# DeltaNet's element-wise work off GpSimd, and its projections summed in one set of PSUM columns

## The chip, the cores and the metric

The kernel runs on one core of a Trainium2 chip. The metric is the device time of one execution in microseconds (us); the time before is the median of three runs. TensorE (PE) multiplies, VectorE (DVE) and ScalarE (ACT) do element-wise work from SBUF and PSUM, GpSimd (POOL) does element-wise work in SBUF and issues its own DMAs, and SyncE (SP) issues the loads of the weights.

## What is computed

One decoder block on 256 tokens of width 2048: an input norm, two mixers side by side (sparse attention, NSA, and a gated DeltaNet), gates that merge them, an output projection with a residual, a SwiGLU feed-forward and a last norm. The change touches DeltaNet alone, whose reference, cut to what matters, is this:

```python
def gated_deltanet(qkv, z, a, beta_logit, conv_w, a_log, dt_bias, norm_w):
    qkv = silu(causal_depthwise_conv(qkv, conv_w))          # 4 taps
    q, k, v = split into 8 heads of 128
    q = l2norm(q) * dk ** -0.5
    k = l2norm(k)
    gc = jnp.cumsum(chunks(gdec), axis=-1)
    decay = jnp.exp(jnp.where(lower_incl, gc[..., :, None] - gc[..., None, :], -jnp.inf))
    lmat = jnp.where(strict, jnp.einsum('bhnid,bhnjd->bhnij', kb, k) * decay, 0.0)
    tinv = lax.linalg.triangular_solve(eye + lmat, eye, left_side=True, lower=True)
    ...
    o = rms_norm(o, norm_w) * jax.nn.silu(z)
```

## The kernel before

**The weight stream.** Nearly all the time goes into products of 256 tokens with some 270 MB of weights. The weights come in chunks of 1 MB (`load`, L122, three buffers `raw`). Each half of a chunk is split by `split` (L133) in two parts for the reduced-precision matmul: ScalarE copies `hi` (L141), VectorE subtracts to get `lo` (L142), with three buffers of each. The activations are kept as `hi` and `lo` parts too. A product is the sum of hi·hi, hi·lo and lo·hi. `group_t` (L180) makes 256 output columns, transposed, out of two chunks: for each piece of 128 rows and each of two feature tiles, one matmul of 512 columns multiplies the weights' `hi` with both parts of the activations (L196), and one of 256 columns the weights' `lo` with the activations' `hi` (L197). A half-chunk has eight such pairs. The two sums stand in different PSUM columns, so ScalarE copies the one to SBUF (L200, `ev`) and VectorE adds the other to it (L202).

**The lanes.** The mixers are written as generators. After every half-chunk, `pump` takes one more piece from each of three lanes, so that the mixers' work stands between the weights' products. `split` is issued at a raised priority, so that `hi` and `lo` stand ahead of the mixers' work on ScalarE and VectorE where they can; `pin` keeps an instruction no earlier on its engine than where it is written. Each engine works through its own list in order: a waiting instruction holds up all behind it.

**DeltaNet.** Six groups of 512 features (k, k, v, v, q, q; L1054 and after), each two calls of `group_t`, are scaled by the input norm's factor into `pre` (`conv_in`, L344). `conv_taps` (L347) takes the first of four taps as a product (L353) and adds three (L355), all on VectorE, then ScalarE applies silu. `dn_small` makes the decay factors `E` on GpSimd (subtraction, mask before the exponential and mask after it, L326, L327, L335); `prep_k` multiplies them by 1/|k| (L390) and with the keys' products into `MT` (L402). `solve` inverts 64 diagonal blocks of 32 x 32: the blocks go through DRAM (`scrM`) into `Lb` with a block on each partition; GpSimd masks the rest of `MT` (L430), scales `Lb` (L435), takes 31 steps of a product (L441) and a difference (L443), and copies the transpose (L446); the inverses go back through DRAM (`scrT`, `scrTT`) into `D` and `DT`. `dn_main` waits for all of it, multiplies the gate `zs` by the output norm's weight on GpSimd (L510), and makes the products `P`, `U` and the state's. `dn_norm` scales the output and multiplies it by the gate on GpSimd (L636), and `dn_out` transposes it into `odn`.

**After it.** NSA's keys and queries go through `rope` (L655) on GpSimd. Later stages (merge gates, output projection, feed-forward) use the same `group_t` and `group` and aren't changed.

Of the kernel before, what the change touches and what calls it, by code (L numbers as in the profile page):

```python
# [14 lines left out]
P = 128  # L15
# [78 lines left out]
class Kern:  # L94
# [50 lines left out]
    def group(self, srcs, acts, w=512, first=None, t_outer=False):  # L145
        """one group of w output columns, tokens on partitions: out[tok, w] in ps[t][:, :w]

        t_outer: the last three half-chunks serve the first 128 tokens before the others."""
# [31 lines left out]
    def group_t(self, srcs, acts, out=None):  # L180
        """one group of 256 output columns, transposed: out[f*128.., tok] is the sum of
        ps[:, f, 0, :] (both products with the hi parts of the activations) and ps[:, f, 1, :]"""
# [21 lines left out]

    def hilo(self, out, v):
        """out[:, 0] + out[:, 1] = v, in two parts for the products"""
        self.hilo2(out[:, 0], out[:, 1], v)
# [19 lines left out]
    def rsqrt(self, v, shape, tag):  # L227
        """1/sqrt(v) in float32: a first guess from the bits and Newton steps."""
# [10 lines left out]
    def pin(self, ins):  # L239
        """no earlier on its engine than where it is written"""  # L240
        return self.tc.keep_in_program_order(ins)
# [8 lines left out]
    def bc(self, col, n):  # L250
        """[P, a] -> [P, a, n]"""
        a = col.shape[1]
        return col.unsqueeze(2).to_broadcast([P, a, n])

    # ================= DeltaNet =================
    def dn_small(self, ab):
# [47 lines left out]
        # decay factors, transposed: E[j, i] = exp(gc_i - gc_j) for i >= j, else 0  # L304
        up = self.cs["utri"][:, None, :].to_broadcast([P, 4, 128])
# [13 lines left out]
        for i in range(len(order) + 3):  # L319
            if i < len(order):  # L320
# [3 lines left out]
                if t == 0:  # L324
                    self.pin(nc.gpsimd.tensor_tensor(self.kd[:, hs], E[:, :, 127], self.gc[:, 0, hs], op=OP.subtract))
                self.pin(nc.gpsimd.tensor_tensor(E.ap, E.ap, self.bc(self.gc[:, t, hs], 128), op=OP.subtract))  # L326
                self.pin(nc.gpsimd.tensor_tensor(E.ap, E.ap, up, op=OP.mult))  # L327
            if i >= 3:
                t, hg = order[i - 3]
# [5 lines left out]
                self.pin(nc.gpsimd.tensor_tensor(E.ap, E.ap, up, op=OP.mult))  # L335
            yield

    def conv_in(self, e, half, pre):
        """rows of a group, scaled, where the causal conv reads them: [128 ch, 4, 3 + 256 tok]"""
# [7 lines left out]
    def conv_taps(self, pre, cT, feat0):  # L347
        """causal conv over 4 feature tiles, then silu"""
        nc, V = self.nc, self.nc.vector
        cw = self.sm["cw"]  # L350
        for f in range(4):
            o = (feat0 + f) * 4
            V.tensor_scalar(cT[:, f, :], pre[:, f, 0:256], cw[:, o:o + 1], None, op0=OP.mult)  # L353
# [9 lines left out]
    def prep_k(self, pre, cT, hg):  # L363
# [14 lines left out]
        # 1/|k| goes into the decay factors, the row scales and the keys for the state  # L378
# [9 lines left out]
        for t in range(2):  # L388
            E = self.E[t, hg]
            nc.gpsimd.tensor_tensor(E.ap, E.ap, self.bc(rk[:, t, :], 128), op=OP.mult)  # L390
# [14 lines left out]
    def solve(self):  # L405
        """inverses of the 32x32 diagonal blocks of I + L, blocks on partitions"""
# [22 lines left out]
        # off-diagonal blocks only, for the products  # L429
        nc.gpsimd.tensor_tensor(self.MT.ap, self.MT.ap, self.cs["offmask"][:, None, :].to_broadcast([P, 16, 128]), op=OP.mult)  # L430
# [4 lines left out]
        nc.gpsimd.tensor_tensor(Lb[:64], Lb[:64], bb[:64, None, :].to_broadcast([64, 32, 32]), op=OP.mult)  # L435
        yield
        prf = pr[:64].rearrange("p a b -> p (a b)")
        for j in range(31):
            n, m = 31 - j, j + 1
            pv = prf[:, :n * m].rearrange("p (a b) -> p a b", b=m)  # L440
            nc.gpsimd.tensor_tensor(pv, Lb[:64, j, j + 1:32].unsqueeze(2).to_broadcast([64, n, m]),  # L441
                            Tb[:64, j, 0:m].unsqueeze(1).to_broadcast([64, n, m]), op=OP.mult)
# [876 lines left out]
```

## Time and profile before

| what | value |
|---|---|
| median of 3 runs | 1530.34 us (1530.16 to 1530.35) |
| span of the profiled execution, first to last instruction | 1526.5 us |
| TensorE matmul, busy | 1491.8 us (98%) |
| VectorE, busy | 989.9 us (65%) |
| ScalarE, busy | 713.1 us (47%) |
| GpSimd, busy | 248.8 us (16%) |

How to read the rows below. A row of waits has the engine and tile that waited, then the one waited for, and the time in all, the number of times and the longest, in us. A row of windows has the window (us from the span's start), its length, then the busy time (and number of instructions) of TensorE's matmuls, its weight loads, VectorE, ScalarE and GpSimd, the granted TensorE clock as a share of the full one, the DMA share and GB/s. A row of a timeline has the start, the duration, engine, line, operation, output and inputs, the shape and the number; in brackets the idle time before it and what ended it. A row of groups has line, engine, operation, output and inputs, shapes and number, then the busy time in us and the mean of one in ns, then the idle time before them. A matmul's end is modelled, so starts tell more than durations.

### The profile page before, as it was taken

How to read it: one execution, taken by the hardware profiler on the slowest of the kernel's cores; microseconds unless marked ns; L12 is line 12 of the kernel's file. 1: busy time of each engine (PE TensorE's matmuls, PEld its weight loads, DVE VectorE, ACT ScalarE, POOL GpSimd, SP SyncE). 2: the span in 40 equal slices, each digit the busy share in tenths (PEclk: the TensorE clock that was granted, in tenths of full speed). 3: DMA queues.
4: the chain of work that ended last, by engine and by line, in shares of the span. 5: the costliest groups of instructions: out<-in, count | busy, mean ns of one | idle time of the engine just before them, and what ended most of it. 6: DMA issues, size and time to landing. Idle time of an engine off the chain costs nothing.

```text
span 1526.5 us, 20516 instructions
## 1 busy us (share of the span) xinstructions
PE 1491.8 (98%) x8199; PEld 1290.8 (85%) x8199; DVE 989.9 (65%) x1321; ACT 713.1 (47%) x910; POOL 248.8 (16%) x197
## 2 busy tenths in 40 slices
PE   6999999999999999999999999999999999999997
PEld 6988778988888888888888888888888888888886
DVE  7688998578877865676666555555565555455444
ACT  4654433344455545554454444444444444344343
POOL 5140695233500000030000000000000000000000
PEclk8999999999999999999999999999999999999999
DMA  6645446335654455555545555555555555555553
GB/s 230 220 170 184 145 146 190 114 138 184 231 182 152 155 187 181 183 181 189 185 174 193 192 180 183 190 193 180 182 190 193 180 183 217 193 193 194 193 193 110
DMA packets 40943, 276.74 MB, mean 181 GB/s; under 512 B 4992, under 2 KB 5008, under 8 KB 9232
## 3 DMA queue, kind: packets, MB, share of 16 engines
q1 hardware_dynamic: 38592, 268.34, 50.5%
q10 hardware_dynamic: 1152, 4.46, 0.8%
q0 software_dynamic: 1104, 2.64, 0.7%
q8 instruction: 64, 1.05, 0.3%
q14 instruction: 31, 0.25, 0.0%
HBM read 272.52 MB, written 2.89 MB: 180 GB/s over the span
## 4 chain that ended last, share of the span: by engine, by line
PE 90%; DVE 6%; POOL 1%; issue 1%; ACT 1%; DMA 0%; SPq 0%; DVEq 0%; ACTq 0%; POOLq 0%
PE mm L196 40%; PE mm L197 20%; PE mm L218 8%; PE mm L219 8%; PE mm L217 8%; DVE lo L142 3%; DVE main L355 1%; PE U L534 1%; PE oacc L862 1%; ACT hi L141 0%; POOL main L662 0%; DMA xs<-in_xT 0%; PE pt L848 0%; POOL ys L664 0%; DVE zsg L344 0%
## 5 line engine op out<-in xcount | busy, mean ns | idle before, releaser
L142 DVE TENSOR_TENSOR lo<-raw,hi 128x1024 fp32r<-128x1024 f32 (+2 forms) x512 | 649.4, 1271 | 468.6 <-ACT hi L141 464.1
L141 ACT ACTIVATE hi<-raw 128x1024 fp32r<-128x1024 f32 (+2 forms) x512 | 535.5, 1047 | 735.6 <-PE mm L196 430.1
L196 PE MATMUL mm<-h,hi 128*128 128x512 f32 x1408 | 497.7, 397 | 0.0
L196 PE MATMUL mm<-hh,hi 128*128 128x512 f32 x1152 | 415.1, 402 | 0.0
L197 PE MATMUL mm<-h,lo 128*128 128x256 f32 x1408 | 395.8, 281 | 0.0
L197 PE MATMUL mm<-hh,lo 128*128 128x256 f32 x1152 | 326.0, 283 | 11.1 <-DVE lo L142 11.0
L196 PEld LDWEIGHTS mm<-h,hi 128*128 128x128 f32 x1408 | 264.7, 188 | 65.2
L197 PEld LDWEIGHTS mm<-h,lo 128*128 128x128 f32 x1408 | 264.3, 188 | 0.0
L196 PEld LDWEIGHTS mm<-hh,hi 128*128 128x128 f32 x1152 | 217.9, 189 | 50.5 <-issue 0.2
L197 PEld LDWEIGHTS mm<-hh,lo 128*128 128x128 f32 x1152 | 217.7, 189 | 14.2 <-DVE lo L142 14.0
L1167 POOL TENSOR_TENSOR sgt<-sgt,R 128x512 f32<-128x512 f32 x22 | 39.5, 1798 | 544.4 <-ACT sgt L1166 544.4
L219 PE MATMUL mm<-hi,fxy 128*128 128x512 f32 x192 | 75.6, 394 | 0.0
L218 PE MATMUL mm<-lo,fxy 128*128 128x512 f32 x192 | 75.3, 392 | 0.0
L217 PE MATMUL mm<-hi,fxy 128*128 128x512 f32 x192 | 74.5, 388 | 0.0
L219 PE MATMUL mm<-hi,fa 128*128 128x512 f32 x160 | 63.0, 394 | 0.0
L218 PE MATMUL mm<-lo,fa 128*128 128x512 f32 x160 | 62.7, 392 | 0.0
L217 PE MATMUL mm<-hi,fa 128*128 128x512 f32 x160 | 62.1, 388 | 0.0
L202 DVE TENSOR_TENSOR ev<-mm,ev 128x512 f32<-128x512 f32 x88 | 60.1, 683 | 0.0
L1106 POOL TENSOR_TENSOR main<-main 128x512 f32<-128x512 f32 x7 | 14.1, 2015 | 267.3 <-DVE main L1105 267.3
L200 ACT ACTIVATE ev<-mm 128x512 f32<-128x512 f32 x96 | 55.9, 582 | 0.0
L217 PE MATMUL mm<-hi,hh 128*128 128x354 f32 (+2 forms) x128 | 46.8, 366 | 5.8 <-ACT hh L972 5.8
L218 PE MATMUL mm<-lo,hh 128*128 128x354 f32 (+2 forms) x128 | 46.4, 362 | 6.0 <-DVE lo L142 6.0
(345 smaller groups left out, 1698.7 us busy)
## 6 DMA issues: line engine op xcount, KB each, us to landing
raw<-in_wfg SPq DMA_DIRECT2D x88, 1024.0 KB, 4.8
raw<-in_wd SPq DMA_DIRECT2D x44, 1024.0 KB, 4.8
raw<-in_wmg SPq DMA_DIRECT2D x32, 1024.0 KB, 4.9
raw<-in_wdn SPq DMA_DIRECT2D x24, 1024.0 KB, 4.9
raw<-in_nsa SPq DMA_DIRECT2D x16, 1024.0 KB, 4.9
raw<-in_wo SPq DMA_DIRECT2D x16, 1024.0 KB, 4.8
raw<-in_wud SPq DMA_DIRECT2D x8, 1024.0 KB, 4.8
raw<-in_wun SPq DMA_DIRECT2D x8, 1024.0 KB, 4.9
```

The costliest lines, as they stand in the source:

```text
L141: nc.scalar.activation(hv, rv[:, m * h:m * h + m, :], AF.Copy)
L142: nc.vector.tensor_tensor(lv, rv[:, m * h:m * h + m, :], hv.bitcast(F32), op=OP.subtract)
L196: nc.tensor.matmul(ps[:, f], hv[:, k, fs], a, start=begin, stop=False, skip_group_check=True)
L197: nc.tensor.matmul(ps[:, f, 0, :], lv[:, k, fs], a[:, 0, :], start=False, stop=last, skip_group_check=True)
L200: nc.scalar.activation(e[:], ps[:, :, 1, :], AF.Copy)
L202: nc.vector.tensor_tensor(out, ps[:, :, 0, :], e[:], op=OP.add)
L217: nc.tensor.matmul(o, a[:, 0, sl], hv[:, k, :], start=begin, stop=False)
L218: nc.tensor.matmul(o, a[:, 0, sl], lv[:, k, :], start=False, stop=False)
L219: nc.tensor.matmul(o, a[:, 1, sl], hv[:, k, :], start=False, stop=last)
L355: V.scalar_tensor_tensor(cT[:, f, :], pre[:, f, j:j + 256], cw[:, o + j:o + j + 1], cT[:, f, :], op0=OP.mult, op1=OP.add)
L534: nc.tensor.matmul(bv[:, j, :], Pm[t, hg][:, j, :], U[t, hg][:, j, :], start=True, stop=True)
L1167: nc.gpsimd.tensor_tensor(sgt[:], sgt[:], self.R2b, op=OP.mult)
```

## The change

- The decay factors are made on VectorE, one head at a time: a subtraction and a minimum with zero in one instruction, then the exponential on ScalarE. The masks go; the mask is applied once, in the product with 1/|k|.
- In the solve, the mask of `MT` (in four pieces, one per half-chunk), the scaling of `Lb` and the 62 steps move to VectorE, with more yields between the steps, and the transposed copy moves to ScalarE.
- The gate's product with the norm's weight goes; the weight is brought onto the partitions as `dnwc` and applied where `dn_out` evacuates the transposed output. In `dn_norm`, scale and gate are one VectorE instruction per head.
- DeltaNet's projections use `group_s`: three products of 256 columns into the same PSUM columns, with no addition after them; `conv_in` reads PSUM.
- The first tap of the convolution is an activation on ScalarE.
- `rope` may take its buffer from another free region.

```diff
+    def group_s(self, srcs, acts):
+        ps = self.pmain.tile([P, 2, 256], F32, tag="mm", name=self.nm("mm"))
...
+                    for f in range(2):
+                        fs = slice(f * P, f * P + P)
+                        nc.tensor.matmul(ps[:, f], hv[:, k, fs], a[:, 0, :], start=begin and f == 0, stop=False, skip_group_check=True)
+                        nc.tensor.matmul(ps[:, f], hv[:, k, fs], a[:, 1, :], start=False, stop=False, skip_group_check=True)
+                        nc.tensor.matmul(ps[:, f], lv[:, k, fs], a[:, 0, :], start=False, stop=last, skip_group_check=True)
+                self.pump()
+        return ps[:]
...
-        for i in range(len(order) + 3):
+        for i in range(len(order) + 1):
...
-                self.pin(nc.gpsimd.tensor_tensor(E.ap, E.ap, self.bc(self.gc[:, t, hs], 128), op=OP.subtract))
-                self.pin(nc.gpsimd.tensor_tensor(E.ap, E.ap, up, op=OP.mult))
+                for j in range(4):
+                    h = hg * 4 + j
+                    self.pin(V.tensor_scalar(E[:, j, :], E[:, j, :], self.gc[:, t, h:h + 1], 0.0, op0=OP.subtract, op1=OP.min))
...
                 self.pin(nc.scalar.activation(E.ap, E.ap, AF.Exp))
-                self.pin(nc.gpsimd.tensor_tensor(E.ap, E.ap, up, op=OP.mult))
...
-            V.tensor_scalar(cT[:, f, :], pre[:, f, 0:256], cw[:, o:o + 1], None, op0=OP.mult)
+            self.pin(nc.scalar.activation(cT[:, f, :], pre[:, f, 0:256], AF.Copy, scale=cw[:, o:o + 1]))
...
-            nc.gpsimd.tensor_tensor(E.ap, E.ap, self.bc(rk[:, t, :], 128), op=OP.mult)
+            for j in range(4):
+                V.scalar_tensor_tensor(E[:, j, :], E[:, j, :], rk[:, t, j:j + 1], self.cs["utri"], op0=OP.mult, op1=OP.mult)
...
-        nc.gpsimd.tensor_tensor(self.MT.ap, self.MT.ap, self.cs["offmask"][:, None, :].to_broadcast([P, 16, 128]), op=OP.mult)
...
-        nc.gpsimd.tensor_tensor(Lb[:64], Lb[:64], bb[:64, None, :].to_broadcast([64, 32, 32]), op=OP.mult)
+        for q in range(4):
+            self.pin(V.tensor_tensor(self.MT[:, 4 * q:4 * q + 4, :], self.MT[:, 4 * q:4 * q + 4, :],
+                                     self.cs["offmask"][:, None, :].to_broadcast([P, 4, 128]), op=OP.mult))
+            yield
+        self.pin(V.tensor_tensor(Lb[:64], Lb[:64], bb[:64, None, :].to_broadcast([64, 32, 32]), op=OP.mult))
...
-            nc.gpsimd.tensor_tensor(pv, Lb[:64, j, j + 1:32].unsqueeze(2).to_broadcast([64, n, m]),
-                            Tb[:64, j, 0:m].unsqueeze(1).to_broadcast([64, n, m]), op=OP.mult)
-            nc.gpsimd.tensor_tensor(Tb[:64, j + 1:32, 0:m], Tb[:64, j + 1:32, 0:m], pv, op=OP.subtract)
-            if j % 2 == 2 - 1:
+            self.pin(V.tensor_tensor(pv, Lb[:64, j, j + 1:32].unsqueeze(2).to_broadcast([64, n, m]),
+                                     Tb[:64, j, 0:m].unsqueeze(1).to_broadcast([64, n, m]), op=OP.mult))
+            self.pin(V.tensor_tensor(Tb[:64, j + 1:32, 0:m], Tb[:64, j + 1:32, 0:m], pv, op=OP.subtract))
+            if j % 2 or 7 < j < 23:
                 yield
-        nc.gpsimd.tensor_copy(pr[:64], Tb[:64].rearrange("p a b -> p b a"))
+        self.pin(nc.scalar.activation(pr[:64], Tb[:64].rearrange("p a b -> p b a"), AF.Copy))
...
-        zv = self.zs.ap.rearrange("p t (h d) -> p (t h) d", d=128)
-        self.pin(nc.gpsimd.tensor_tensor(zv, zv, self.sm["dnw"][:, None, :].to_broadcast([P, 16, 128]), op=OP.mult))
+        V.tensor_tensor(dg.ap, self.sm["dnw"], self.cs["ident"], op=OP.mult)
+        V.tensor_reduce(self.dnwc[:], dg.ap, axis=AX.X, op=OP.add)
...
-        V.tensor_tensor(o.ap, o.ap, self.bc(r[:], 128), op=OP.mult)
-        nc.gpsimd.tensor_tensor(o.ap, o.ap, self.zs[:, t, hg * 512:hg * 512 + 512].rearrange("p (a b) -> p a b", b=128), op=OP.mult)
+        for j in range(4):
+            V.scalar_tensor_tensor(o[:, j, :], o[:, j, :], r[:, j:j + 1], self.zs[:, t, hg * 512 + j * P:hg * 512 + (j + 1) * P], op0=OP.mult, op1=OP.mult)
...
-        nc.scalar.activation(oh, bv, AF.Copy)
-        V.tensor_tensor(ol, bv, oh.bitcast(F32), op=OP.subtract)
+        nc.scalar.activation(oh, bv, AF.Copy, scale=self.dnwc[:])
+        V.scalar_tensor_tensor(ol, bv, self.dnwc[:], oh.bitcast(F32), op0=OP.mult, op1=OP.subtract)
...
-        t = self.ar.alloc([2, 256])
+        t = self.ar.alloc([2, 256], "my")
...
-                e = self.group_t([t["wdn"][(g * 2 + half) * 2 + c] for c in range(2)], hact)
+                e = self.group_s([t["wdn"][(g * 2 + half) * 2 + c] for c in range(2)], hact)
```

**Where instructions move.** VectorE in the middle of the solve, before: the first taps (L353), the additions of the evacuation (L202), and no solve.

```order
L142 TENSOR_TENSOR lo_1851<-raw_1816,hi_1850 128x1024
L142 TENSOR_TENSOR lo_1885<-raw_1882,hi_1884 128x1024
L202 TENSOR_TENSOR ev_1811<-mm_1698,ev_1811 128x512
L344 TENSOR_TENSOR zsg<-ev_1811,R_427 128x2x256
L353 TENSOR_SCALAR main<-zsg,smalls 128x256
L142 TENSOR_TENSOR lo_1910<-raw_1882,hi_1909 128x1024
```

The same stretch of VectorE now (L365 is `conv_in`, L466 and L468 are a step's product and difference, L376 the later taps):

```order
L142 TENSOR_TENSOR lo_2315<-raw_2253,hi_2314 128x1024
L376 SCALAR_TENSOR_TENSOR main<-zsg,smalls,main 128x256
L466 TENSOR_TENSOR xs<-xs 64x256
L364 MEMSET zsg 128x4x3
L365 TENSOR_TENSOR zsg<-mm_2108,R_427 128x2x256
L142 TENSOR_TENSOR lo_2347<-raw_2344,hi_2346 128x1024
L468 TENSOR_TENSOR xs<-xs 64x16x16
L466 TENSOR_TENSOR xs<-xs 64x255
L468 TENSOR_TENSOR xs<-xs 64x15x17
L466 TENSOR_TENSOR xs<-xs 64x252
L468 TENSOR_TENSOR xs<-xs 64x14x18
L142 TENSOR_TENSOR lo_2377<-raw_2344,hi_2376 128x1024
```

Up to five steps of the solve now stand between two `lo`, and `conv_in` takes its operand from the PSUM tile `mm`. Earlier on VectorE, where the blocks have just been sent to DRAM, now (L457 is a piece of the mask of `MT`, L460 the scaling of `Lb`; the pieces of the mask wait for the DMAs that read `MT`, and L460 for those that fill `Lb` and `bb`):

```order
L457 TENSOR_TENSOR main<-main,consts 128x512
L142 TENSOR_TENSOR lo_1862<-raw_1819,hi_1861 128x1024
L457 TENSOR_TENSOR main<-main,consts 128x512 x3
L142 TENSOR_TENSOR lo_1904<-raw_1901,hi_1903 128x1024
L460 TENSOR_TENSOR xs<-xs,bb_1664 64x1024
L365 TENSOR_TENSOR zsg<-mm_1684,R_427 128x2x256
L142 TENSOR_TENSOR lo_1937<-raw_1901,hi_1936 128x1024
```

Before, both stood on GpSimd (L430, L435), with no `lo` behind them. GpSimd from the blocks' stores to those of the inverses, now (L690 to L693 are a rope, L472 and L473 store the inverses):

```order
L449 DMA scrM<-main 32x16x32
L440 DMA bb_1664<-main 16x32 x4
L449 DMA scrM<-main 32x16x32 x3
L450 DMA xs<-scrM 64x1024
L690 TENSOR_TENSOR ys<-ys,consts 64x512
L691 TENSOR_TENSOR ys<-ys,consts 64x512
L692 TENSOR_TENSOR ys<-ys,consts 128x512
L693 TENSOR_TENSOR ys<-ys 128x512
L472 DMA scrT<-xs 64x1024
L473 DMA scrTT<-xs 64x1024
```

Before, the mask, the scaling, the 62 steps and the copy stood between the load of `xs` and the stores, and the first rope came after them. On TensorE the products of the inverses, `P`, come behind the sixty-fourth and sixty-fifth half-chunk after the start of the projections, and before behind the fifty-eighth and fifty-ninth.

## Rows read from the trace of the kernel before

**Rows 1.** Waits of TensorE, whole span.

```profile
PE mm L197 <- DVE lo L142: 11.0, 7, 2.5
...
PE vn L551 <- DVE main L580: 1.6, 1, 1.6
```

**Rows 2.** Windows: projections and solve, the feed-forward, two pieces of low clock.

```profile
68.70:247.60 178.90, 167.89 (x958) 145.33 (x958) 161.02 (x238) 79.69 (x91) 96.30 (x102) 0.98 0.50 172
...
800.00:1200.00 400.00, 400.00 (x2266) 347.37 (x2265) 230.58 (x232) 186.13 (x213) 30.97 (x17) 1.00 0.54 187
...
94.07:97.48 3.41, 3.41 (x11) 2.92 (x12) 3.38 (x4) 0.00 (x0) 1.01 (x1) 0.50 0.00 0
...
213.53:216.94 3.41, 3.41 (x14) 3.03 (x13) 2.96 (x5) 3.22 (x4) 3.25 (x3) 0.50 0.29 50
```

**Rows 3.** Timeline of TensorE, feed-forward, first and fourth pair.

```profile
899.39 0.40 PE L196 MATMUL mm<-h,hi 128*128 128x512 f32 x1
...
900.45 0.40 PE L196 MATMUL mm<-h,hi 128*128 128x512 f32 x1
```

**Rows 4.** Groups of TensorE, 68.7 to 247.6 us.

```profile
L196 PE MATMUL mm<-hh,hi 128*128 128x512 f32 x432 | 156.5, 404 | 0.0
```

**Rows 5.** The chain that ended last, one piece: start, length, what.

```profile
261.37 1.78 PE P L518 x16
```

**Rows 6.** Timeline of VectorE, 170.5 to 178 us.

```profile
170.66 5.97 DVE L142 TENSOR_TENSOR lo<-raw,hi 128x1024 fp32r<-128x1024 f32 x1 [0.40 <-ACT hi L141]
```

**Rows 7.** Timeline of GpSimd, the same stretch.

```profile
170.93 4.62 POOL L430 TENSOR_TENSOR main<-main,consts 128x2048 f32<-128x2048 f32 x1
176.58 2.40 POOL L435 TENSOR_TENSOR xs<-xs,bb 64x1024 f32<-64x1024 f32 x1 [1.03 <-DMA xs<-scrM]
```

**Rows 8.** Groups of VectorE, 68.7 to 247.6 us.

```profile
L142 DVE TENSOR_TENSOR lo<-raw,hi 128x1024 fp32r<-128x1024 f32 x55 | 75.8, 1381 | 15.7 <-ACT hi L141 15.4
L355 DVE SCALAR_TENSOR_TENSOR main<-zsg,smalls,main 128x256 f32<-128x256 f32 x48 | 30.8, 665 | 0.2
...
L344 DVE TENSOR_TENSOR zsg<-ev,R 128x512 f32<-128x512 f32 x12 | 10.9, 911 | 0.4
L353 DVE TENSOR_SCALAR main<-zsg,smalls 128x256 f32<-128x256 f32 x16 | 10.6, 671 | 0.2
L202 DVE TENSOR_TENSOR ev<-mm,ev 128x512 f32<-128x512 f32 x12 | 8.2, 680 | 0.0
```

**Rows 9.** Groups of VectorE, 800 to 1200 us.

```profile
L142 DVE TENSOR_TENSOR lo<-raw,hi 128x1024 fp32r<-128x1024 f32 x142 | 174.0, 1226 | 168.4 <-ACT hi L141 168.4
```

**Rows 10.** Groups of VectorE, whole span.

```profile
L805 DVE TENSOR_TENSOR main<-sc,consts 128x256 f32<-128x256 f32 x8 | 3.3, 416 | 0.0
L797 DVE TENSOR_TENSOR main<-sc,consts 128x15 f32<-128x15 f32 x16 | 2.8, 174 | 10.0 <-PE sc L784 9.9
```

**Rows 11.** Line L815: durations in ns, least, median, greatest.

```profile
L815 DVE TENSOR_SCALAR main<-main,asm x32: 278/308/355, 449.2 to 553.0; 128x128 f32<-128x128 f32 x16, 128x256 f32<-128x256 f32 x16
```

**Rows 12.** Timeline of VectorE, a tap while GpSimd is idle.

```profile
125.38 0.47 DVE L355 SCALAR_TENSOR_TENSOR main<-zsg,smalls,main 128x256 f32<-128x256 f32 x1
```

**Rows 13.** Timeline of TensorE: first of three matmuls of 256 columns; what follows.

```profile
495.37 0.28 PE L782 MATMUL sc<-zkh,zq 128*128 128x256 f32 x1
...
495.72 0.38 PE L848 MATMUL pt<-consts,main 128*128 128x128 f32 x2
```

**Rows 14.** Groups of GpSimd, 68 to 262 us.

```profile
L443 POOL TENSOR_TENSOR xs<-xs 64x31 f32<-64x31 f32 (+15 forms) x31 | 28.8, 928 | 2.4
L441 POOL TENSOR_TENSOR xs<-xs 64x31 f32<-64x31 f32 (+15 forms) x31 | 22.4, 723 | 2.4
```

**Rows 15.** Groups of ScalarE by shape, 440 to 560 us.

```profile
L811 ACT ACTIVATE main<-main,amx 128x256 f32<-128x256 f32 x16 | 8.0, 501 | 11.4 <-DVE amx L809 11.4
```

**Rows 16.** Timeline of GpSimd: start of the first rope and of the second.

```profile
295.48 1.99 POOL L661 TENSOR_TENSOR main<-ys,consts 64x512 f32<-64x512 f32 x1 [33.20 <-PE U L534]
...
302.47 1.26 POOL L661 TENSOR_TENSOR main<-ys,consts 64x512 f32<-64x512 f32 x1
```

More of the change, by code (lines that the diff above doesn't have):

```diff
@@ L203, in group_t @@
         return out
+    def group_s(self, srcs, acts):
+        nc = self.nc
+        ps = self.pmain.tile([P, 2, 256], F32, tag="mm", name=self.nm("mm"))
+        n = len(srcs)
+        for c, src in enumerate(srcs):
+            rv = self.load(src, 256, nk=8)
+            for h in range(2):
+                hv, lv = self.split(rv, 256, h)
+                for k in range(4):
+                    a = acts(c * 8 + h * 4 + k)
+                    begin = c == 0 and h == 0 and k == 0
+                    last = c == n - 1 and h == 1 and k == 3
+                    for f in range(2):
[5 more added lines that the diff above has]
+        return ps[:]
     def hilo(self, out, v):
@@ L303, in dn_small @@
         yield
-        up = self.cs["utri"][:, None, :].to_broadcast([P, 4, 128])
         for _ in range(3):
@@ L324, in dn_small @@
                 if t == 0:
-                    self.pin(nc.gpsimd.tensor_tensor(self.kd[:, hs], E[:, :, 127], self.gc[:, 0, hs], op=OP.subtract))
-                self.pin(nc.gpsimd.tensor_tensor(E.ap, E.ap, self.bc(self.gc[:, t, hs], 128), op=OP.subtract))
-                self.pin(nc.gpsimd.tensor_tensor(E.ap, E.ap, up, op=OP.mult))
-            if i >= 3:
-                t, hg = order[i - 3]
+                    self.pin(V.tensor_tensor(self.kd[:, hs], E[:, :, 127], self.gc[:, 0, hs], op=OP.subtract))
+                for j in range(4):
+                    h = hg * 4 + j
+                    self.pin(V.tensor_scalar(E[:, j, :], E[:, j, :], self.gc[:, t, h:h + 1], 0.0, op0=OP.subtract, op1=OP.min))
+            if i:
+                t, hg = order[i - 1]
                 hs = slice(hg * 4, hg * 4 + 4)
@@ L508, in dn_main @@
             yield
-        zv = self.zs.ap.rearrange("p t (h d) -> p (t h) d", d=128)
-        self.pin(nc.gpsimd.tensor_tensor(zv, zv, self.sm["dnw"][:, None, :].to_broadcast([P, 16, 128]), op=OP.mult))
+        dg = ar.alloc([128], "xm")
+        self.dnwc = self.small([1], "dnwc")
+        V.tensor_tensor(dg.ap, self.sm["dnw"], self.cs["ident"], op=OP.mult)
+        V.tensor_reduce(self.dnwc[:], dg.ap, axis=AX.X, op=OP.add)
+        dg.free()
         Pm, U = {}, {}
```

## The prediction

> **What bounds the kernel now.** I read the busy shares first, then TensorE's waits, then one stretch in windows. TensorE is busy for 98% of the span, but a busy TensorE can hide waits between its matmuls, so the list of its waits comes next: between the projections' products it waited seven times for `lo`, the low parts of the weights that VectorE makes, 11.0 us in all [rows 1]. All seven lie in 68.7 to 247.6 us, the stretch of DeltaNet's projections, convolutions and solve. In its window VectorE is busy for 161.0 of 178.9 us and GpSimd for 96.3, while between 800 and 1200 us VectorE has 230.6 of 400 [rows 2]. So this one stretch is bound by VectorE, and the rest by TensorE.
>
> What a stretch free of waits would take follows from counts. A pair of products, 512 and 256 columns, comes every 0.353 us (three pairs from 899.39 to 900.45) [rows 3]. The stretch holds 432 pairs [rows 4], 152.7 us. The other 94 of its 958 matmuls [rows 2] have 128 columns but for one; sixteen such took 1.78 us elsewhere [rows 5], so 10.4 us. That is 163.1 us; the stretch takes 178.9, so 15.8 us are lost. The parts agree: 11.0 us of waits, and two pieces of 3.41 us in which the granted clock is 0.50, so 1.2 GHz instead of 2.4 [rows 2]. Each follows a wait. The first holds 11 matmuls, 5.5 pairs, which at the full clock would take 1.9 us: 1.5 us lost. I take the same for the second. Each wait also hides some 0.16 us in the modelled end of the matmul ahead of it, seven times. Together 15.2 us. This is what the change can win here.
>
> Why VectorE is late: one `lo` took 5.97 us [rows 6] while GpSimd ran the 4.62 us mask product of L430 [rows 7]. Operations with two operands in SBUF are slow beside GpSimd: `lo` takes 1.381 us on average in the stretch [rows 8] against 1.226 later [rows 9]; a tap (L355) takes 0.665 against 0.47 [rows 8, 12]. L202, which has an operand in PSUM, stays at 0.680 [rows 8]. The excess: 55 x 0.155 for `lo`, 48 x 0.195 for the taps into `main`, 12 x 0.23 for L344 (against the 0.68 of L202, the same size), 16 x 0.316 for the first taps (L353, against the 0.355 of L815 at 256 columns [rows 11]): 8.5 + 9.4 + 2.8 + 5.1 = 25.8 us. The Trainium skill ("SBUF — State Buffer", Who interferes with whom) says that a VectorE instruction with two SBUF inputs and a GpSimd instruction that reads SBUF block each other for the whole instruction; these rows agree.
>
> **The change, part by part.**
>
> *GpSimd.* In the stretch it keeps only DMA issues and, near its end, one rope. The excess of 25.8 us goes.
>
> *Evacuation and first tap.* Twelve additions of 0.68 us (L202) leave VectorE, 8.2 us, and L344 reads PSUM at the same price. Twenty-four first taps leave at their undisturbed 0.355, 8.5 us. ScalarE gets 24 activations of 256 columns at 0.50 [rows 15], 12 us, and loses 12 copies; it is busy for 79.7 of 178.9 us [rows 2], which covers that. Without the cover `hi` would be late, and with it `lo`.
>
> *Solve.* 62 products and differences come to VectorE, with 10,912 elements a partition. No row shows them there. By the nearest rows, 0.174 us for 15 columns and 0.416 for 256 [rows 10], a step costs 0.159 + 0.0010 per element, 20.8 us in all. The low end is 16.5: neighbours that don't depend on each other overlap by 0.07. The high end is GpSimd's own 28.8 + 22.4 = 51.2 us [rows 14]. I take 20.8, since engine and sizes are those of the rows. The work added beside it: 16 subtractions at 0.28 [rows 11], 16 products with the mask at 0.28 to 0.47, say 0.36 [rows 11, 12], four off-mask pieces at 0.68 [rows 8], one product of 1,024 at 1.23 [rows 9], small ones 0.8. That makes 15.0, with the solve 35.8 us.
>
> *VectorE's sum:* 161.0 - 25.8 - 16.7 + 35.8 = 154.3 us, against TensorE's 163.1. TensorE becomes the bound, with 5% to spare. The order puts up to five solve steps between two `lo`, so some pieces are longer than the 2.83 us of a half-chunk (eight pairs). Two waits for DMAs now stand on VectorE, ahead of `lo`: the first mask piece for the stores of the blocks and the product on `Lb` for its load. GpSimd, which waited for the same two, began L430 at 170.93 and L435 at 176.58, 5.65 us later [rows 7]. VectorE has two `lo` and four mask pieces from the one to the other, 5.2 us. Last, the first rope on GpSimd now comes before the solve's stores and lies beside its last steps; a rope takes 7.0 us [rows 16]. For all of these I leave 4 us of waits, between 0 and the present 15.2.
>
> *The stores after the solve* wait for that rope. They are covered: the products with `D` come six half-chunks (17 us) later in TensorE's order than before.
>
> *Three products of 256 columns* instead of 512 and 256, in 384 places. Three such matmuls with new weights each start 0.35 us from first to next (495.37 to 495.72) [rows 13]; the pair takes 0.353. That is 0 to -0.003 us each; I take -0.8 us in all.
>
> *Later:* the gate's factor and four GpSimd products in the output norm go to VectorE and ScalarE after the stretch, where TensorE's one wait of note is 1.6 us [rows 1]; nothing counted. What covers them there is VectorE's spare time; without it each of the sixteen products of 128 columns would cost its 0.28 to 0.47 us.
>
> **Sum.** The profiled span is 1526.5 us; the median of the runs is 1530.34, so 3.8 lie around the span. 1526.5 - 15.2 + 4 - 0.8 = 1514.5, with 3.8 it is **1518.3 us**. About 0.2%, 3.1 us, is what a measurement here can tell from no change: same is 1527.3 to 1533.4.
>
> **Rivals.**
>
> 1. *Half of the gain is lost to new waits on VectorE* (masks and `Lb` behind DMAs, long pieces, the rope). For it: only 5% to spare, and two of the seven waits brought a piece of slow clock with them. Against: `hi` and `lo` have three buffers each, so TensorE has some two half-chunks, 5.7 us, in hand. With 10 us left: 1524.3. Chance 0.17.
>
> 2. *VectorE stays the bound, as much as now:* the solve costs what GpSimd's absence gives. That needs VectorE at 174 to 180 us, a solve near 45. 1527.3 to 1533. Chance 0.08.
>
> 3. *Slower: the solve's steps are dear on VectorE.* The steps form a chain of broadcast operands; at GpSimd's prices VectorE needs 154.3 + 30.4 = 184.7 us, 5.8 more than the stretch takes now: 1530.3 + 5.8 - 0.8 = 1535.3. It decides from a mean step of 0.73 us on (45.4 us), where 0.34 follows from the rows. Against: the order sets taps and `lo` between dependent steps. Chance 0.10.
>
> 4. *Each matmul has a price of its own.* At 2.4 GHz 768 columns are 320 ns, the pair takes 353; if the 33 ns were per matmul, a third costs 16.5 ns more, 6.3 us in 384 places: 1525.4 by my sum. Against: [rows 13], where three take no more than the pair. Chance 0.06. The Trainium skill ("TensorE: Matmul & The Clock Gate", Back-to-back issue gap) gives a sustained 81 ns at 128 columns and 131 at 512 for pairs of weight load and matmul; an estimate between these makes the triple 65 ns dearer, 25 us, 1543. The trace differs from that page: 0.353 for the pair.
>
> **How the numbers follow.** The forecast (most of the stalls go, 0 to 7 us stay) has 0.59: 1514 to 1522. Faster is 0.59 + 0.17 + 0.06 = 0.82, same 0.08, slower 0.10. The low end, 1511, is no stall left in the stretch, the 1.6 us wait gone too and 1 us more. The high end, 1529, takes in rivals 1 and 4 and the start of rival 2, and leaves out rival 3.
>
> **What would show it.** Right: TensorE's wait for `lo` falls from 11.0 us to under 4, the two slow pieces of clock are gone, `lo` takes 1.23 us throughout, L202 and L353 are gone from the stretch, solve steps take 0.17 to 0.42, and the triple takes 0.35. Wrong: VectorE over 95% busy through the stretch with TensorE still waiting 8 us or more (rivals 1 to 3; the mean of a solve step tells which), VectorE idle at the masks behind a DMA, or a triple over 0.36 us (rival 4).

## The result and the profile after

The change makes the kernel faster: 1515.43 us median of 4 runs (1514.16 to 1516.09) against 1530.28 (1530.16 to 1530.35). The ratio is 0.9916, 95% interval [0.9903, 0.9929]. The profiled execution took 1514.85 us, its span is 1513.1 us, so 13.4 us less span than before.

TensorE's waits of the changed kernel, 60 to 1400 us (engine, what waited, for what: us in all, times, longest), where [rows 1] had 11.0 in seven and 1.6 more:

```profile
PE mm L197 <- DVE lo L142: 5.3, 5, 3.4
```

The windows of [rows 2], changed kernel:

```profile
68.70:247.60 178.90, 178.26 (x1429) 173.86 (x1429) 157.16 (x328) 91.86 (x113) 18.14 (x24) 1.00 0.55 184
800.00:1200.00 400.00, 400.00 (x2310) 351.59 (x2309) 234.05 (x235) 189.76 (x217) 32.87 (x18) 1.00 0.56 190
```

In the first window GpSimd is down from 96.3 to 18.1 us, the clock is at 1.00, and TensorE is busy to the brim. VectorE's 157.2 are not to be set against 161.0 directly, because the window now holds more of the program. The second window holds a surprise: 2310 matmuls instead of 2266 in 400 us, in a stage that the change doesn't touch.

VectorE's groups in the first window, changed kernel (line, operation, shapes, number, then busy us, mean ns, idle before), which answer to [rows 8, 14]:

```profile
L142 DVE TENSOR_TENSOR lo<-raw,hi 128x1024 fp32r<-128x1024 f32 x58 | 72.0, 1242 | 16.3 <-ACT hi L141 16.3
L376 DVE SCALAR_TENSOR_TENSOR main<-zsg,smalls,main 128x256 f32<-128x256 f32 x48 | 21.0, 471 | 0.1
L468 DVE TENSOR_TENSOR xs<-xs 64x31 f32<-64x31 f32 (+15 forms) x31 | 12.4, 399 | 0.3
L466 DVE TENSOR_TENSOR xs<-xs 64x31 f32<-64x31 f32 (+15 forms) x31 | 12.2, 395 | 0.4
...
L365 DVE TENSOR_TENSOR zsg<-mm,R 128x512 f32<-128x512 f32 x12 | 8.1, 678 | 0.1
```

`lo` is at 1.24 us instead of 1.381, a tap at 0.471 instead of 0.665, `conv_in` at 0.678 instead of 0.911. The solve's 62 steps take 24.6 us on VectorE; on GpSimd they took 51.2.

**Where the waits are now.** Of the 5.3 us, 0.9 lie in the stretch of the forecast. The other 4.4 are new, at 372 and 379 us, where the kernel before had no wait for `lo` (only 0.4 us for something else, at 377 us). VectorE there, changed kernel (start, us, engine, line, operation):

```profile
367.83 0.85 DVE L255 TENSOR_TENSOR ro_u<-ro_y 128x4 f32<-128x4 f32 x1
...
368.92 1.15 DVE L257 SCALAR_TENSOR_TENSOR ro_y<-ro_u,ro_y 128x4 f32<-128x4 f32 x1
...
370.20 2.30 DVE L142 TENSOR_TENSOR lo<-raw,hi 128x1024 fp32r<-128x1024 f32 x1
372.43 5.41 DVE L665 SCALAR_TENSOR_TENSOR main<-main,ro_y 128x128 f32<-128x128 f32 x4
377.76 3.43 DVE L142 TENSOR_TENSOR lo<-raw,hi 128x1024 fp32r<-128x1024 f32 x2
```

GpSimd in the same microseconds, with the rotations of NSA's queries:

```profile
367.38 1.28 POOL L690 TENSOR_TENSOR main<-main,consts 64x512 f32<-64x512 f32 x1 [89.27 <-DVE ro_y L257]
368.72 1.32 POOL L691 TENSOR_TENSOR main<-main,consts 64x512 f32<-64x512 f32 x1
...
373.73 1.29 POOL L690 TENSOR_TENSOR main<-main,consts 64x512 f32<-64x512 f32 x1
375.07 1.27 POOL L691 TENSOR_TENSOR main<-main,consts 64x512 f32<-64x512 f32 x1
```

TensorE's timeline at the second wait, and the window of slow clock behind it:

```profile
375.24 0.40 PE L196 MATMUL mm<-hh,hi 128*128 128x512 f32 x1
379.02 0.46 PE L197 MATMUL mm<-hh,lo 128*128 128x256 f32 x1 [3.38 <-DVE lo L142]
```

```profile
379.19:382.60 3.41, 3.41 (x12) 2.92 (x13) 3.41 (x2) 0.00 (x0) 3.25 (x3) 0.50 0.74 240
```

An operation on four columns takes 1.15 us, and ends when GpSimd's step does (370.04 us). Four products of the output norm (L665, one per head), 0.34 us each when alone, take 5.41 us: one in turn with each step of a rotation. `lo` stands behind them.

**Where the 13.4 us came from.** Matmuls of the unchanged stages, kernel before: number, least, median and greatest ns, first and last start. The first row is the gate and up products of the feed-forward, the second the products on DeltaNet's output, the third the feed-forward's last products:

```profile
L196 PE MATMUL mm<-h,hi x1408: 389/397/482, 776.5 to 1275.0; 128*128 128x512 f32 x176
...
L196 PE MATMUL mm<-odn,hi x128: 397/397/398, 595.2 to 640.1; 128*128 128x512 f32 x128
...
L217 PE MATMUL mm<-hi,fa x160: 388/388/392, 1275.3 to 1516.4; 128*128 128x512 f32 x160
```

The same of the changed kernel:

```profile
L196 PE MATMUL mm<-h,hi x1408: 392/392/476, 767.1 to 1256.4; 128*128 128x512 f32 x176
...
L196 PE MATMUL mm<-odn,hi x128: 392/397/402, 584.2 to 629.1; 128*128 128x512 f32 x128
...
L238 PE MATMUL mm<-hi,fa x160: 393/396/397, 1256.8 to 1502.5; 128*128 128x512 f32 x160
```

Up to the products on `odn` the change has gained 11.0 us (595.2 to 584.2). From there to 776.5 it loses 1.6 (181.3 to 182.9), in the gate stage it gains 9.1 (498.8 to 489.7), and in the last stage it loses 5.1 (251.2 to 256.3). So 11.0 us are the change's work, and 2.4 net are stages whose code is the same: from the first product on `odn` to the end of the span the kernel before takes 931.3 us and the changed one 928.9. The experiments below differ in these stages too, and their times have to be read with that.

### The profile page after: what moved, and what is told of

It reads as the page before. It is cut to its first block, busy times and chain, and to the rows that moved or that the text cites. A ratio compares the mean times of both kernels' runs of the same rounds, so it can differ in the third digit from the quotient of the medians.

```text
span 1513.1 us, 21295 instructions
## 1 busy us (share of the span) xinstructions
PE 1485.2 (98%) x8583; PEld 1303.0 (86%) x8583; DVE 971.9 (64%) x1400; ACT 719.7 (48%) x923; POOL 147.6 (10%) x109
## 4 chain that ended last, share of the span: by engine, by line
PE 95%; DVE 3%; DMA 0%; issue 0%; ACT 0%; SPq 0%; DVEq 0%; ACTq 0%
PE mm L196 36%; PE mm L197 18%; PE mm L239 9%; PE mm L240 9%; PE mm L238 9%; PE mm L221 3%; PE mm L222 3%; PE mm L220 3%; DVE lo L142 1%; PE oacc L891 1%; PE U L563 1%; DMA raw<-in_zab 0%; PE pt L877 0%; DVE xs L468 0%; DVE main L376 0%
## 5 line engine op out<-in xcount | busy, mean ns | idle before, releaser
L142 DVE TENSOR_TENSOR lo<-raw,hi 128x1024 fp32r<-128x1024 f32 (+2 forms) x512 | 635.1, 1242 | 471.4 <-ACT hi L141 470.0
L196 PE MATMUL mm<-h,hi 128*128 128x512 f32 x1408 | 488.6, 392 | 0.0
L196 PE MATMUL mm<-hh,hi 128*128 128x512 f32 x768 | 276.5, 401 | 0.0
L196 PEld LDWEIGHTS mm<-hh,hi 128*128 128x128 f32 x768 | 145.1, 189 | 33.4 <-issue 0.2
L220 PE MATMUL mm<-hh,hi 128*128 128x256 f32 x384 | 108.7, 283 | 0.0
L221 PE MATMUL mm<-hh,hi 128*128 128x256 f32 x384 | 107.9, 281 | 0.0
L220 PEld LDWEIGHTS mm<-hh,hi 128*128 128x128 f32 x384 | 72.4, 188 | 0.0
L221 PEld LDWEIGHTS mm<-hh,hi 128*128 128x128 f32 x384 | 72.4, 189 | 0.0
L238 PE MATMUL mm<-hi,fa 128*128 128x512 f32 x160 | 63.2, 395 | 0.0
```

The lines of the kernel that those rows point to most:

```text
L142: nc.vector.tensor_tensor(lv, rv[:, m * h:m * h + m, :], hv.bitcast(F32), op=OP.subtract)
L196: nc.tensor.matmul(ps[:, f], hv[:, k, fs], a, start=begin, stop=False, skip_group_check=True)
L220: nc.tensor.matmul(ps[:, f], hv[:, k, fs], a[:, 0, :], start=begin and f == 0, stop=False, skip_group_check=True)
L221: nc.tensor.matmul(ps[:, f], hv[:, k, fs], a[:, 1, :], start=False, stop=False, skip_group_check=True)
L238: nc.tensor.matmul(o, a[:, 0, sl], hv[:, k, :], start=begin, stop=False)
```

## The experiments

In these runs the kernel before had medians of 1528.3 to 1528.9 us, so the ratio to it is what to compare; the changed kernel's is 0.9916. Theory C says that TensorE stalls where GpSimd's work stretches VectorE's; theory S, that only VectorE's total counts.

| kernel | median us | ratio to before, 95% interval |
|---|---|---|
| changed, solve back on GpSimd | 1517.36 | 0.9927 [0.9912, 0.9942] |
| changed, pairs and first tap back | 1518.76 | 0.9936 [0.9919, 0.9953] |
| before, three products and tap alone | 1518.62 | 0.9944 [0.9922, 0.9965] |
| changed, idle GpSimd work, early | 1521.17 | 0.9950 [0.9935, 0.9965] |
| changed, idle GpSimd work, in the solve | 1535.70 | 1.0049 [1.0033, 1.0065] |
| before, tiles 32 bytes on | 1524.20 | 0.9971 [0.9960, 0.9983] |
| changed, tiles 32 bytes further | 1513.27 | 0.9902 [0.9881, 0.9924] |
| changed, norm's product on GpSimd | 1511.68 | 0.9892 [0.9875, 0.9908] |
| before, rotations on VectorE | 1526.81 | 0.9990 [0.9981, 0.9999] |
| changed, rotations on VectorE | 1506.37 | 0.9854 [0.9838, 0.9871] |
| the same, tile of 64 bytes | 1505.13 | 0.9850 [0.9834, 0.9866] |
| the same, tile of 128 bytes | 1515.55 | 0.9917 [0.9898, 0.9936] |

**The solve back on GpSimd.**

```diff
-            self.pin(V.tensor_tensor(pv, Lb[:64, j, j + 1:32]...
-            self.pin(V.tensor_tensor(Tb[:64, j + 1:32, 0:m], ...
+            self.pin(nc.gpsimd.tensor_tensor(pv, Lb[:64, j, j + 1:32]...
+            self.pin(nc.gpsimd.tensor_tensor(Tb[:64, j + 1:32, 0:m], ...
```

The off-mask (one operation again) and the product on `Lb` go back too.

> The changed kernel with the solve's 62 steps, the off-mask and the product on Lb back on GpSimd; all else as changed. Theory C (what stalls TensorE is a `lo` stretched while GpSimd computes): `lo` lies near 1.4 us beside the steps and up to 6 us beside the mask, TensorE waits 6 us or more for `lo`, 1521 to 1528 us. Theory S (only VectorE's sum of busy time against TensorE's time counts): VectorE loses 28.5 us of solve and gains about 0.31 us for each of GpSimd's 58 us, 18 us, so its sum falls to about 147 us in the stretch, and the time is 1513 to 1516 us.

1517.4 us lies between the theories. The ratio is 0.0011 above the changed kernel's, 1.7 us, and the intervals overlap: by the medians the largest piece of the diff is worth little. But part of its worth is hidden by stages whose code is the same: from the first product on `odn` to the end this kernel takes 926.9 us (589.1 to 1516.0) where the changed one takes 928.9. Up to that product it is 4.9 us behind (589.1 to 584.2). By the medians, 1.7 and 2.0 us, the solve's move is worth some 4 us. Its waits and what made them (VectorE, then GpSimd, whose L456 and L457 are the off-mask and the product on `Lb`):

```profile
PE mm L222 <- DVE lo L142: 4.2, 2, 2.6
```

```profile
164.84 7.40 DVE L376 SCALAR_TENSOR_TENSOR ys<-zsg,smalls,ys 128x256 f32<-128x256 f32 x1
```

```profile
165.00 4.62 POOL L456 TENSOR_TENSOR main<-main,consts 128x2048 f32<-128x2048 f32 x1
169.58 2.38 POOL L457 TENSOR_TENSOR xs<-xs,bb 64x1024 f32<-64x1024 f32 x1
```

One tap took 7.40 us: GpSimd ran two long operations back to back and the tap came after both. That is C's mechanism. The longer wait, 2.6 us, came of these two operations, with a piece of slow clock behind it; the 62 short steps brought only the other, of 1.5 us. With room on VectorE, short GpSimd operations cost little.

**Either half alone.** The changed kernel with both of VectorE's reliefs taken back, and the kernel before with nothing but them:

```diff
-                e = self.group_s([t["wdn"]...], hact)
+                e = self.group_t([t["wdn"]...], hact)
...
-            self.pin(nc.scalar.activation(cT[:, f, :], pre[:, f, 0:256], AF.Copy, scale=...))
+            V.tensor_scalar(cT[:, f, :], pre[:, f, 0:256], cw[:, o:o + 1], None, op0=OP.mult)
```

> The changed kernel with the pairs, the copy and the addition back in the projections, and the first tap back on VectorE; GpSimd stays silent there. Theory C: `lo` stays at 1.24 us, waits stay under 5 us in the stretch, 1516 to 1520 us. Theory S: VectorE gets back 16.7 us, is busy for 174 us where TensorE needs some 166, and the time is 1525 to 1531 us.

> The kernel before, with only the three products in the same columns and the first tap on ScalarE (the complement of the run with both taken back). Theory C: GpSimd's work stays, `lo` stays at 1.38 us, TensorE still waits 8 us or more, 1523 to 1529 us. Theory S: VectorE loses 16.7 us and falls to 144 us, the waits nearly vanish, 1515 to 1518 us.

The first, 1518.8 us, bears out C. The second, 1518.6 us, lies just above S's range, and its waits between the two theories, so neither holds alone. The profiled execution of the first is the fastest of its ten (1513.5 us). Windows of the first and of the second:

```profile
68.70:247.60 178.90, 178.60 (x1058) 156.71 (x1057) 167.07 (x345) 86.72 (x100) 13.72 (x14) 1.00 0.54 181
```

```profile
68.70:247.60 178.90, 171.97 (x1394) 167.99 (x1393) 151.17 (x220) 87.66 (x111) 100.79 (x103) 0.98 0.55 179
```

With GpSimd silent, VectorE can be 93% busy and TensorE hardly waits, at least in that execution: of the first row below only 0.7 us lie near the stretch, at 251 us, and the rest is the wait at 372 to 380 us again. The second row, at 266 us, is for the inverses of a solve that ends later.

```profile
PE mm L197 <- DVE lo L142: 5.2, 3, 3.4
PE P L547 <- DMA wsg<-scrT: 1.7, 1, 1.7
```

With VectorE at 85% and GpSimd busy, three waits of TensorE for `lo` stay (two in this row, and one of 1.2 us), 6.9 us of the 11.0, and a clock of 0.98:

```profile
PE mm L222 <- DVE lo L142: 5.7, 2, 4.2
```

The ratios make the halves look like substitutes: 0.9936 and 0.9944 alone are 9.8 and 8.6 us, and 0.9916 together is 12.9. But TensorE's pace outside the two halves is in these numbers. Products on `odn` of the first and of the second, whose spans end at 1511.6 and 1517.0 us:

```profile
L196 PE MATMUL mm<-odn,hi x128: 392/392/392, 584.8 to 628.9; 128*128 128x512 f32 x128
```

```profile
L196 PE MATMUL mm<-odn,hi x128: 397/397/398, 585.4 to 630.3; 128*128 128x512 f32 x128
```

From there to the end the first takes 926.8 us and the second 931.6, against 931.3 before. The first thus owes 4.5 us to stages that it doesn't touch, the changed kernel 2.4, the second nothing (it loses 0.3). And the second's three products run at a faster pace than the pair, worth 3 us, while the changed kernel's cost 0.8 us (see the part on the prediction). Taken out, 5.3 and 5.9 us are left, and 11.3 together: by this estimate, from one profile each and with intervals of 2 to 3 us either way, the halves simply add up. In the fastest execution of the first, 1513.5 us, nothing is left for the second half to gain (the changed kernel takes 1514.2 to 1516.1); over its ten there is. The first scatters from 1513.5 to 1527.1 us over ten runs, as a stage with no slack would; that this is why was not tried.

**Idle work on GpSimd.**

```diff
+            self.pin(nc.gpsimd.tensor_tensor(jk[:64, :n * m], ..., op=OP.mult))
+            self.pin(nc.gpsimd.tensor_tensor(jk[:64, :n * m], ..., op=OP.subtract))
```

> The changed kernel with 62 additional operations on GpSimd that nobody reads, of the sizes of the solve's steps and beside them, some 50 us. If GpSimd's work stretches VectorE's by itself (about 0.31 us for each us, from the 25.8 us of excess in the kernel before), VectorE takes some 15 us more in the stretch, `lo` beside it 1.5 us, and the time is 1519 to 1526 us. If the excess in the kernel before came from something else, the time stays within 1 us of 1515.4.

These operations waited for nothing and ran from 30 to 76 us, before the solve: they delayed the start, and tell nothing of the stretch. The next run makes them read `Lb`.

> The changed kernel with 62 additional operations on GpSimd that nobody reads, held back until the solve's blocks are there, so that they lie beside the projections as the solve's steps did in the kernel before. If GpSimd's work stretches VectorE's by itself (0.31 us for each us, from the 25.8 us of excess in the kernel before): some 50 us of GpSimd, 15 us more on VectorE, `lo` beside it 1.5 us, TensorE waits 4 to 8 us more: 1519 to 1525 us. If it does not: within 1.5 us of the changed kernel.

1535.7 us: 20 more than the changed kernel, far over the range. VectorE and GpSimd in some of its microseconds:

```profile
198.01 0.81 DVE L467 TENSOR_TENSOR xs<-xs 64x247 f32<-64x247 f32 x1
198.75 0.83 DVE L376 SCALAR_TENSOR_TENSOR main<-zsg,smalls,main 128x256 f32<-128x256 f32 x1
199.51 0.40 DVE L469 TENSOR_TENSOR xs<-xs 64x247 f32<-64x247 f32 x1
199.83 1.21 DVE L142 TENSOR_TENSOR lo<-raw,hi 128x1024 fp32r<-128x1024 f32 x1
200.97 0.47 DVE L376 SCALAR_TENSOR_TENSOR main<-zsg,smalls,main 128x256 f32<-128x256 f32 x1
```

```profile
198.63 0.67 POOL L470 TENSOR_TENSOR jk<-xs,ones 64x255 f32<-64x255 f32 x1
199.38 2.53 POOL L471 TENSOR_TENSOR jk<-xs,ones 64x255 f32<-64x255 f32 x1
```

The two engines take turns by whole operations: a step of 0.41 us takes 0.81, a tap of 0.47 takes 0.83. Then a step, `lo` and a tap run one behind the other at their undisturbed 0.40, 1.21 and 0.47, and it is GpSimd's step that takes 2.53. `lo` itself is not stretched (1.216 us on average, not the 1.5 expected); the steps and taps in front of it are, and so it comes late. A price per microsecond of GpSimd (my 0.31) misses that. The waits in which it shows:

```profile
PE mm L222 <- DVE lo L142: 10.2, 5, 5.7
...
PE qtr L511 <- ACT main L380: 3.5, 1, 3.5
```

But not all of the 20 us come of taking turns. The longest wait, 5.7 us at 227 us, has another cause: VectorE stood idle for 10.2 us ahead of it.

```profile
224.53 0.29 DVE L540 TENSOR_TENSOR xs<-smalls,consts 128x128 f32<-128x128 f32 x1 [10.20 <-POOL jk L471]
```

L540, a product for the gate's factor, waited until the last of the idle operations was done. It writes into the region `xs`, where `Lb` lies, which all 62 read; that this is the reason is likely and was not tried. So the experiment made this wait itself. With the slow clock behind it (0.51 from 224.7 to 231.5 us) it is worth some 8 us, an estimate. That leaves some 12 us for the turns, still more than the 3.6 to 9.6 that I had expected.

**The new wait at 372 to 382 us.** First the norm's product back on GpSimd:

```diff
-            V.scalar_tensor_tensor(o[:, j, :], o[:, j, :], r[:, j:j + 1], self.zs[...], ...)
+        V.tensor_tensor(o.ap, o.ap, self.bc(r[:], 128), op=OP.mult)
+        nc.gpsimd.tensor_tensor(o.ap, o.ap, self.zs[...], op=OP.mult)
```

> The changed kernel with the output norm's product with the gate back on GpSimd (four products of 512 columns, and VectorE's four scalings by the row factor, as in the kernel before). Theory C: the changed kernel's new wait at 371 to 379 us (4.8 us in two, and 3.4 us of slow clock) comes from that product having been moved to VectorE, beside a rotation on GpSimd; on GpSimd it stands in one queue with the rotations, the wait falls under 1 us and the slow piece goes: 1508 to 1511 us. Rival: the wait comes from the rotations themselves, which now lie beside other work of VectorE; then it stays within 1 us, 1514 to 1517 us.

```profile
PE mm L197 <- DVE lo L142: 3.3, 4, 2.3
```

1511.7 us: the longest wait falls from 3.4 to 2.3 us and the slow clock stays. Theory C was half right; the rotations beside `lo` and the four-column steps make the rest. Taking the rotations themselves away:

```diff
-        G = self.nc.gpsimd
+        G = self.nc.vector
```

> The changed kernel with the rotations of NSA's queries and keys on VectorE instead of GpSimd. Theory C puts the changed kernel's wait of 5.0 us at 371 to 379 us, and the slow clock of 3.4 us after it, down to the output norm's products, now on VectorE, being stretched from 0.34 to 1.35 us beside a rotation on GpSimd: both vanish, VectorE takes 2.7 us for each of seven rotations where TensorE has time to spare, 1508 to 1511 us. If VectorE's own load there is what holds `lo` up, the wait stays or grows: 1515 to 1520 us.

1506.4 us, and no wait of TensorE is left between 60 and 1400 us. The solve's steps, beside whose end the first rotation stood, give back 4.2 us as well:

```profile
L468 DVE TENSOR_TENSOR xs<-xs 64x31 f32<-64x31 f32 (+15 forms) x31 | 10.2, 329 | 0.2
L466 DVE TENSOR_TENSOR xs<-xs 64x31 f32<-64x31 f32 (+15 forms) x31 | 10.2, 328 | 0.3
```

> The kernel before with the rotations on VectorE, all else as before. If the 9 us that this gained in the changed kernel are the undoing of a wait that the change itself had made, the kernel before, which has no such wait there (0.4 us at 377 us), gains little: the 248 us stall behind the first rotations and some of the 1.6 us wait, 1526 to 1530 us. If rotations on GpSimd cost this program 9 us whatever else it does: 1519 to 1521 us.

1526.8, as the first case said: in the kernel before, the same edit is worth 1.5 us (0.9990). So the wait belongs to the change, which put VectorE's work beside rotations that had cost only those 1.5 us before.

**Where the tiles lie.** The changed kernel has one more small tile, the gate's factor `dnwc`, and everything allocated behind it, the activations too, lies 32 bytes further on.

```diff
+        self.pad = self.small([1], "pad")
+        V.memset(self.pad[:], 0.0)
```

> The kernel before with one more small tile of one column, written once and never read; it moves the activations and all tiles that are allocated behind it by 32 bytes a partition, as the new tile of the gate's factor does in the changed kernel. Theory A (part of the gain is that move: in the feed-forward, which the change does not touch, the 512-column matmul starts its successor after 229 ns in the changed kernel and after 235 in the kernel before): the 512-column step falls to 229 ns from about 775 us on, 1,430 pairs gain 6 ns each, 8.5 us, 1520 to 1523 us. If the step belongs to the program's other changes instead, it stays at 235 ns and the time within 1.5 us of the kernel before.

```profile
L196 PE MATMUL mm<-h,hi x1408: 392/392/476, 774.5 to 1263.8; 128*128 128x512 f32 x176
...
L217 PE MATMUL mm<-hi,fa x160: 393/396/397, 1264.2 to 1509.9; 128*128 128x512 f32 x160
```

The gate stage takes 489.7 us (774.5 to 1264.2), as in the changed kernel, and the last 255.9 (to the span's end, 1520.1). In all 4.1 us less than before, half of what I expected, because the last stage loses what I had not looked at. So the move alone repeats the 9.1 us that the changed kernel gains in the gate stage and nearly the 5.1 that it loses in the last (here 4.7); it does not repeat the 1.6 between the products on `odn` and the gate stage, which takes 181.2 us here (593.3 to 774.5). The other way round, `dnwc` made wider:

```diff
-        self.dnwc = self.small([1], "dnwc")
+        self.dnwc = self.small([16], "dnwc")[:, 0:1]
```

> The changed kernel with the tile of the gate's factor made 64 bytes wide, so that the activations lie again at a multiple of 64 bytes, as in the kernel before. Theory A: the 512-column step is 235 ns again, which costs 8.5 us from 775 us on, and the three products of 256 columns take 0.342 us instead of 0.351 (as in the kernel before with the three products alone), which gives back 3.5 us in 384 places: 1519 to 1522 us. If the place of the tiles does not matter: 1515.4, as the changed kernel.

```profile
L196 PE MATMUL mm<-h,hi x1408: 389/398/478, 763.0 to 1261.4; 128*128 128x512 f32 x176
...
L238 PE MATMUL mm<-hi,fa x160: 389/389/403, 1261.7 to 1500.5; 128*128 128x512 f32 x160
```

The expectation of the time was wrong. The gate stage does go back to 498.7 us (763.0 to 1261.7), but the last stage falls to 249.4 (to 1511.1), so the one pays for the other: 1513.3. Two more on top of the rotations on VectorE:

> The changed kernel with the rotations on VectorE and the gate's factor in a tile of 64 bytes (activations at 0 of 128). As the 64 bytes gave the changed kernel 2.1 us: 1504 us, 1502 to 1506. If the place of the activations is worth nothing: 1506.4.

> The same with the factor's tile 128 bytes wide, so that the activations lie at 64 of 128, as in the kernel before. There the three products take 0.342 us (kernel before with the three products) against 0.351 to 0.357 in the changed kernel, 384 places, 4 to 6 us less; the stages from the up projections on take 840.9 us as in the kernel before, against 838.4 in the changed kernel, 2.5 us more: 1503 us, 1501 to 1506.

The first gives 1505.1, the lowest time here: 0.9850 of before, where the change alone has 0.9916 (the rotations alone, at 0.9854, can't be told from it). The second gives 1515.5, 10.4 us more with the same instructions:

```profile
L196 PE MATMUL mm<-h,hi x1408: 388/397/478, 759.3 to 1257.8; 128*128 128x512 f32 x176
...
L238 PE MATMUL mm<-hi,fa x160: 392/396/398, 1258.1 to 1503.8; 128*128 128x512 f32 x160
```

Both have the slow gate stage (498.7 and 498.8 us). The last stage takes 249.0 us in the first (1254.3 to 1503.3) and 256.1 in the second (1258.1 to 1514.2), and 251.2 in the kernel before. So with the activations where they lay in the kernel before, its gate stage comes back and its last stage doesn't, and my reading (the activations' place alone decides) falls. Which tile's place sets which stage stays open.

## Why the prediction was right

The time, 1518.3 forecast and 1515.4 measured, is inside the range, and it came about in the main as the likeliest case had it. Step by step:

- **The stretch is VectorE-bound, and 15.2 us can be won there.** Right. 0.9 us of waits and no slow clock are left in it. With GpSimd silent alone the waits nearly go (in the fastest execution); with VectorE's relief alone 6.9 of the 11.0 us stay.
- **GpSimd is the cause.** Right as one of two. The idle work shows that GpSimd's operations alone can cost some 12 us (an estimate; 8 more are the experiment's own). But the solve's move, which I took for the heart of it, is worth only some 4 us: it takes stretching off VectorE and puts 24.6 us of steps on it. Without it VectorE's sum was already low enough but for two waits. The Trainium skill ("SBUF — State Buffer", Who interferes with whom) has a lock of whole operations; the rows above agree, down to a four-column operation of 1.15 us. My average of 25.8 us of excess was a fair size for the old mixture and no price for another.
- **The solve at 20.8 us.** Right: 20.4 with no rotation beside it, 24.6 with one. Rivals 2 and 3 fall.
- **4 us of waits left, at the masks, at `Lb` and in the long pieces.** This term was mis-placed: 0.9 us in the stretch. The DMAs at the masks cost VectorE under 1 us.
- **"Later: nothing counted."** This step failed. The norm's products moved to VectorE beside the rotations, and 4.4 us of waits came of it, with a piece of slow clock: its 12 matmuls are six pairs, 2.1 us at full clock, so 1.3 us are lost. I looked for VectorE's spare time there and not for what GpSimd was doing in it. 0.9 + 4.4 + 1.3 is 6.6 us where I had 4.
- **Three products for the price of two.** Mis-sized, and not a constant. Timeline of TensorE, the first matmul of one place and of the place three later in the changed kernel, then of one and the place seven later in the kernel before with three products and tap alone:

```profile
104.15 0.28 PE L220 MATMUL mm<-hh,hi 128*128 128x256 f32 x1
...
105.22 0.28 PE L220 MATMUL mm<-hh,hi 128*128 128x256 f32 x1
```

```profile
103.51 0.28 PE L220 MATMUL mm<-hh,hi 128*128 128x256 f32 x1
...
105.89 0.28 PE L220 MATMUL mm<-hh,hi 128*128 128x256 f32 x1
```

  Three places take 1.07 us in the first, 0.357 each; seven take 2.38 in the second, 0.340 each. The second doesn't keep that pace: from its starts of L220, about half of its half-chunks run at 0.340 and the rest at 0.353 or more. Over all places whose step is under 0.4 us the mean is 0.355 in the changed kernel and 0.345 in the second. Against the pair's 0.353 that is +0.8 and -3 us in 384 places, where I had -0.8. Rival 4 (a price per matmul) falls with either.
- **Not in the sum at all:** the 2.4 us net in stages whose code is the same; the place of the tiles accounts for the two larger parts of it, and the 1.6 us stay open. Nor is the 1.6 us wait for `main` of [rows 1], which is gone too. And the 3.8 us around the span were too many: in the profiled execution after they are 1.75, and an execution of the kernel before with a span of 1526.5 took 1528.33. The other 2 were the difference of one execution from the median. The first two made the forecast 4.0 us too long, and what lies around the span 1.5 (the median less the span is 2.3 us after). The 6.6 for 4 and the dearer products made it 4.2 too short. That leaves 1.6 of its 2.9 us unaccounted; the forecast's closeness is partly luck.

## What to carry to other kernels

Before moving work to VectorE, look at what GpSimd does beside its new place, not only at VectorE's idle share there: the two alternate by whole operations, and a four-column step can cost a microsecond. Before saying whether two halves of a change add up, take out of each time the stages that neither touches: here 9.8 and 8.6 us against 12.9 looked like substitutes, and with those stages taken out they add up. An experiment that adds idle work must not read a buffer whose place others need; look at what ended each wait before putting a price to the work. When a kernel changes by some 0.5%, compare the stages that were not touched: a new tile of a few bytes can move them by 9 us, and an edit is easily credited with that.

## What was not expected of the hardware

- Operations of VectorE and GpSimd with two operands in SBUF don't share time, they take turns, and not one for one: one tap waited through two GpSimd operations, 4.62 and 2.38 us, and one GpSimd step of 0.67 us took 2.53 while three VectorE operations ran. The first taps, with one such operand and a column of factors, are stretched too: 0.671 us in the kernel before, 0.343 with GpSimd silent (changed, pairs and first tap back). An operand in PSUM keeps an operation out of it: `conv_in` takes 0.683 us in the kernel before with three products and tap alone, where GpSimd is busy for 100.8 us, and 0.678 in the changed kernel.
- TensorE's pace depends on where tiles lie: in the same 1408 pairs of the gate stage 489.7 or 498.8 us, in the last stage 249.0 to 256.3, and in the changed kernel 0.355 us on average for the three products, with the tile of 64 bytes 0.360 (from the starts of L220). The granted clock was 1.00 in all these products. Which tile sets which pace is open.
